# Attention of a fused two-block kernel: no weight splits on GpSimd, score copies on ScalarE, two heads' score products in turns, and a branch whose short arm comes first

## The chip, the cores and the metric

The kernel runs on one core of a Trainium2 chip. The metric is the time of one execution in device microseconds; of several runs the median counts. The trace is one profiled execution of its own; its engines are PE (TensorE), PEld (its weight loads), DVE (VectorE), ACT (ScalarE), POOL (GpSimd) and SP (SyncE, which issues most of the transfers).

## The reference, cut to what matters

One sequence of 256 positions, 1024 wide, goes through two blocks. The first mixes with a gated delta rule, a sparse attention and a pooling mixer, and has a feed-forward part with 4096 hidden columns. The second is modulated by a condition vector (six vectors of 1024 from `cond @ ada_w`), has a stick-breaking attention of 16 heads of width 64, and a mixture of 32 experts of which each position takes two; a root-mean-square norm ends it. The change is in the attention and behind the experts. What the attention computes:

```python
mod = cond @ ada_w[i] + ada_b[i]
sh1, sc1, g1, sh2, sc2, g2 = jnp.split(mod[:, None, :], N_MOD, axis=-1)
h = rms_norm_2(x, norm_g[i, 0]) * (1.0 + sc1) + sh1
...
z = jnp.einsum('bhqd,bhkd->bhqk', q_blk, k, preferred_element_type=jnp.float32) * scale
causal = kpos[None, :] < qpos[:, None]
log_keep = jnp.where(causal, jax.nn.log_sigmoid(-z), 0.0)
suffix = lax.cumsum(log_keep, axis=3, reverse=True) - log_keep
a = jnp.where(causal, jnp.exp(jax.nn.log_sigmoid(z) + suffix), 0.0)
return jnp.einsum('bhqk,bhkd->bhqd', a.astype(v.dtype), v)
```

## The kernel before, in words

Every large weight is read from memory in tiles of 1 MB into a ring (`ring`, issued on SP). The dense products want nearly full float32 precision, so `split` cuts each weight half-tile of 128x1024 in two parts: `whi`, a rounded copy made by ScalarE (L278), and `wlo = w - whi` (L279), made by VectorE, or, while `self.share` is set, by GpSimd and VectorE in alternation. TensorE then makes three products per piece (hi·hi, lo·hi, hi·lo: L340 to L342 in `dense`, L373 to L375 in `dense_T`, L400 to L402 in `dense_out`). `ffn` sets `self.share` at its very end (L1326), so the splits of the attention alternate.

`stick` is the attention. `proj(c)` runs over six chunks of 512 columns of the input projection in the order v, qk, qk, qk, v, qk. A v chunk leaves `sv` by two VectorE copies (L1373); a qk chunk leaves `sq` by ScalarE (L1378) and `sk` by VectorE (L1379). `score(j)` works on two heads, which lie in rows 0 to 63 and 64 to 127 of one `sq`/`sk` tile. For each head, one after the other, it makes a 256-column product, a 128-column product and adds the mask by a product with the identity (L1387, L1388, L1390). Each head has its own 512 columns of the tile `z`. Then VectorE makes the scaled copy `zs` (L1393), ScalarE makes Abs, Exp and Ln (L1395 to L1397), VectorE makes `ze` (L1398), ScalarE `zehi` (L1400), and GpSimd (for j below 6) or VectorE makes `zelo` (L1401). After that the cumulative sum is a product with a triangular matrix into `c` (L1405 to L1407), VectorE subtracts it (L1408) and ScalarE takes Exp (L1409). `value(j)` multiplies with v (L1418, L1419); here the two heads write different column halves (64 output rows each). `hilo` makes `ohi` and `olo` (L919, L920).

Scores of j = 0 to 5 are made between the projection chunks. Those of j = 6 and 7 are mixed into the output projection (`dense_out`, order of `SB_END`), which is called the tail below. `res` and the sums over squares follow, then routing and the experts.

Beside the attention, the modulation of the second half is made: `self.side` (L1423) holds eight pieces of work (`ada`, quarters 4 and 5, four tiles each), and every weight tile that a dense loop takes pops one entry (`beside`), the first four being empty. A piece is a 1 MB tile and four VectorE operations `ada` (L1218), and the last piece of a quarter adds a few products (L1228).

The order of instructions on each engine is fixed in the program; a scheduler has set it by priority, and in the last part, the tail, it is the order of the code.

The experts' part is called through `If(level < 33)`. The near arm walks 28 positions of experts (each 6 MB of weights) and calls `ends(rest)`: the last sums, the norm, the output (`sums`, `finish`: four transfers, all issued on SP, L2015), then a load of the size of the next position into a register on the engines and a second branch (`If(nv > 0)`, L1983) for the positions that are hardly ever filled. In the traced execution that body is skipped.

Of the kernel before, what the change touches and what calls it, by code (L numbers as in the profile page):

```python
# [8 lines left out]
F32 = mybir.dt.float32  # L9
# [191 lines left out]
class Kern:  # L201
# [1045 lines left out]
    def ffn(self):  # L1247
        nc, a = self.nc, self.a
        with self.tc.tile_pool(name="ffn", bufs=2, reuse_waits="tile") as pool:
# [75 lines left out]
            self.more_split()  # L1325
            self.share = True  # L1326

# [7 lines left out]
    def stick(self):  # L1335
        nc, a = self.nc, self.a
        hT = self.sT
        with self.tc.tile_pool(name="sb", bufs=1, reuse_waits="tile") as pool:
# [23 lines left out]
            def proj(c):  # L1362
                kind, ix = SB_CHUNKS[c]
                off = c * D * 512
                if kind == "v":
                    outs = [self.ps("mm") for _ in range(2)]
                    if c == 0:
                        self.warm(EDGE, "z")
                    self.dense(a["sb_w_in"], off, 512, 2, hT, outs, lead=self.last_T if c == 0 else None)
                    if c == 0:  # L1370
                        self.ordered.close()
                    for i in range(2):
                        nc.vector.tensor_copy(v[ix][i], outs[i])  # L1373
                    return
                outs = [self.ps("mm", (128, 2, T)) for _ in range(2)]
                self.dense_T(a["sb_w_in"], off, 512, hT, outs)
                qT[ix], kT[ix] = [pool.tile([128, 2, T], F32, name=z, bufs=2) for z in ("sq", "sk")]
                nc.scalar.activation(qT[ix], outs[0], AF.Copy)  # L1378
                self.i_proj = nc.vector.tensor_copy(kT[ix], outs[1])  # L1379

            def score(j):

                z = self.ps("z", (128, 2, 512))
                for b in range(2):
                    par = slice(64 * b, 64 * b + 64)
                    q, k = qT[j // 2][par, j % 2], kT[j // 2][par, j % 2]
                    nc.tensor.matmul(z[:, b, 0:256], k[:, 0:128], q, start=True, stop=False)  # L1387
                    nc.tensor.matmul(z[:, b, 256:384], k[:, 128:256], q[:, 128:256], start=False, stop=False)  # L1388
                    zz = z[:, b].rearrange("p (a b) -> p a b", a=4)
                    nc.tensor.matmul(zz[:, 0:3:2], self.identb, self.neg[:, 1:2].to_broadcast([128, 2, 128]), start=False, stop=True)  # L1390
                z = z[:, :, 0:384]
                zs = pool.tile([128, 2, 384], F32, name="zs", tag="zs", bufs=4)
                nc.vector.tensor_scalar(zs, z, 0.125, None, op0=OP.mult)  # L1393
                e = pool.tile([128, 2, 384], F32, name="ze", bufs=2)
                nc.scalar.activation(e, z, AF.Abs, scale=0.125)  # L1395
                nc.scalar.activation(e, e, AF.Exp, scale=-1.0)
# [3 lines left out]
                nc.scalar.activation(hi, e, AF.Copy)  # L1400
                (nc.gpsimd if j < 6 else nc.vector).tensor_sub(lo, e, hi.bitcast(F32))  # L1401
                yield
# [19 lines left out]
            scratch = lambda: pool.tile([128, 2, 384], F32, name="ze", bufs=2).rearrange("p a b -> p (a b)")[:, 0:256]  # L1422
            self.side = [None] * 4 + [lambda q=q, b=b: ada(q, b) for q in (4, 5) for b in range(4)]  # L1423

# [99 lines left out]
    def route(self, pool):  # L1524
# [72 lines left out]
        for i in range(2):  # L1597
# [27 lines left out]
        self.level = c.tile([1, 1], I32, name="level")  # L1625
        nc.vector.scalar_tensor_tensor(self.level, self.eid[:, 1, BIG:BIG + 1], 32.0,
                                       self.eid[:, 1, BIG + MID:BIG + MID + 1], op0=OP.subtract, op1=OP.max)
        self.slot = c.tile([128, 4, NPOS], F32, name="slot")
# [304 lines left out]
    def positions(self):  # L1933
# [4 lines left out]
        for z, p in enumerate(fixed):  # L1938
            self.job(p, 4, self.xg1, 32 * z, z, ("po", "pg"))
        level = nc.values_load(self.level, min_val=-32, max_val=128)  # L1940
        with tc.If(level < 33) as near:
# [9 lines left out]
            self.walk(order, batches, ("po", "pg"))  # L1951
            self.ends(rest)
        with near.Else():
# [48 lines left out]
    def finish(self):  # L2002

        nc, a = self.nc, self.a
        with self.in_order(mybir.EngineType.DVE):
            rstd = [self.rstd(i) for i in range(2)]
            for i, r in enumerate(rstd):
                for n in range(2):
# [4 lines left out]
                    else:  # L2013
                        nc.vector.scalar_tensor_tensor(y, self.x[:, i, cc], r, self.fg[:, cc], op0=OP.mult, op1=OP.mult)
                    nc.sync.dma_start(a["out"][128 * i:128 * i + 128, cc], y)  # L2015

# [52 lines left out]
```

## Time and profile before

| | us |
|---|---|
| runs | 1034.55, 1035.42, 1038.5; median 1035.42 |
| profiled execution | 1031.82 |
| its span, first to last instruction | 1030.0 |
| mean granted clock of TensorE | 0.975 of full speed |
| PE / DVE / ACT / POOL busy | 931.6 / 617.2 / 375.1 / 140.1 |
| attention, from the first v product to the last value product | about 409 to 539 |
| experts | about 560 to 1014 |
| last output transfers issued | 1018.2 to 1022.6 |

The shares of the page are averages over stages with different limits, so each stage is read by itself: which engine is full there, what ends the waits of that engine, and whether a gain there can reach the end.

### The profile page before, as it was taken

The page shows a single profiled execution, that of the slowest core. Times are in us where ns is not written, and L with a number is a line of the kernel's source. Part 1 is how long each engine was busy: PE and PEld are TensorE (multiplying, and loading weights), DVE is VectorE, ACT ScalarE, POOL GpSimd, SP SyncE. Part 2 cuts the span into 40 slices and gives each one's busy share as a digit, 9 for nine tenths or more (in the row PEclk, how much of TensorE's full clock was granted, in tenths as well). Part 3 has the DMA queues.
Part 4 walks back from the last instruction along what each step waited for, and adds up shares of the span by engine and source line. Part 5 has one row for each costly group of instructions (what it writes and reads, how often), then busy time and mean ns, then how long its engine had stood idle before and what let it go on. Part 6 is the DMA issues. An engine that isn't in the chain of part 4 may idle for free.

```text
span 1030.0 us, 16215 instructions
## 1 busy us (share of the span) xinstructions
PE 931.6 (90%) x6318; PEld 618.2 (60%) x6318; DVE 617.2 (60%) x1077; ACT 375.1 (36%) x661; POOL 140.1 (14%) x108
## 2 busy tenths in 40 slices
PE   8999998999999999999898988888788899988873
PEld 6766866778899897997766553333244334434331
DVE  5977767459777655587746764454445252545443
ACT  6574344455445555465452222111122111111112
POOL 4426420201000003444410000000000000000001
PEclk9999999999999999999899999999999999999997
DMA  9641051688968844465748899999999999999992
GB/s 326 233 155 61 23 205 42 244 328 297 393 253 294 316 171 165 170 252 198 269 158 305 314 366 374 423 420 420 420 421 421 422 420 422 419 421 421 421 421 110
DMA packets 47076, 306.74 MB, mean 298 GB/s; under 512 B 6138, under 2 KB 7170, under 8 KB 12040
## 3 DMA queue, kind: packets, MB, share of 16 engines
q1 hardware_dynamic: 46696, 304.43, 75.2%
q8 instruction: 54, 0.88, 0.4%
q10 hardware_dynamic: 288, 1.11, 0.3%
q14 instruction: 38, 0.31, 0.1%
HBM read 304.47 MB, written 1.06 MB: 297 GB/s over the span
## 4 chain that ended last, share of the span: by engine, by line
PE 65%; DMA 16%; DVE 12%; ACT 4%; issue 2%; SPq 0%; POOL 0%; DVEq 0%; ACTq 0%
DMA ring<-in_moe_w_dram 15%; PE t L1787 8%; PE py L1845 5%; PE mm L373 4%; PE mm L374 4%; PE mm L375 4%; PE pg L1783 3%; PE g L340 3%; PE g L341 2%; PE g L342 2%; PE mm L1700 2%; PE po L1875 2%; DVE cacc L667 2%; PE mm L342 1%; DVE ada L1218 1%
## 5 line engine op out<-in xcount | busy, mean ns | idle before, releaser
L278 ACT ACTIVATE whi<-ring 128x1024 fp32r<-128x1024 f32 (+2 forms) x129 | 134.1, 1044 | 113.8 <-PE mm L375 53.8
L279 DVE TENSOR_TENSOR wlo<-ring,whi 128x1024 fp32r<-128x1024 f32 (+2 forms) x99 | 127.5, 1290 | 71.6 <-ACT whi L278 70.5
L1787 PE MATMUL t<-ring,xg 128*32 128x256 f32 (+1 forms) x1632 | 139.6, 409 | 4.4 <-DMA ring<-in_moe_w_dram 4.4
L1787 PEld LDWEIGHTS t<-ring,xg 128*32 128x32 f32 (+1 forms) x1632 | 54.5, 113 | 72.9 <-issue 37.6
L1845 PE MATMUL py<-ring,ht 128*32 128x512 f32 (+2 forms) x488 | 85.1, 628 | 11.8 <-DMA ring<-in_moe_w_dram 7.7
L279 POOL TENSOR_TENSOR wlo<-ring,whi 128x1024 fp32r<-128x1024 f32 (+1 forms) x30 | 73.9, 2464 | 109.6 <-ACT whi L278 94.5
L1868 ACT ACTIVATE yhi<-y 128x512 fp32r<-128x512 f32 x64 | 40.3, 630 | 121.1 <-DVE y L1867 117.8
L1218 DVE SCALAR_TENSOR_TENSOR ada<-ring,cs,ada 128x512 f32<-128x512 f32 x96 | 75.9, 829 | 1.5 <-DMA ring<-in_ada_w_dram 1.5
L1867 DVE TENSOR_TENSOR y<-py,g 128x512 f32<-128x512 f32 x64 | 44.1, 689 | 51.7 <-PE py L1845 51.3
L1812 ACT ACTIVATE silu<-t 128x128 f32<-128x128 f32 (+1 forms) x30 | 8.9, 298 | 166.9 <-PE t L1787 166.9
L2000 POOL TENSOR_TENSOR out<-x,fg 128x512 f32<-128x512 f32 x2 | 2.9, 1448 | 459.8 <-DVE x L1650 459.8
L1650 DVE SCALAR_TENSOR_TENSOR x<-po,slot,x 128x512 f32<-128x512 f32 x63 | 47.1, 748 | 22.5 <-PE po L1875 22.3
L1872 DVE TENSOR_TENSOR ylo<-y,yhi 128x512 fp32r<-128x512 f32 x64 | 44.1, 688 | 24.3 <-ACT yhi L1868 23.6
L1650 DVE SCALAR_TENSOR_TENSOR x<-pg,slot,x 128x512 f32<-128x512 f32 x64 | 46.5, 743 | 7.5 <-PE pg L1875 7.5
L1845 PEld LDWEIGHTS py<-ring,ht 128*32 128x32 f32 (+2 forms) x488 | 20.7, 121 | 48.5 <-issue 33.9
L1813 DVE TENSOR_TENSOR silu<-silu,t 128x128 f32<-128x128 f32 (+1 forms) x30 | 9.4, 313 | 66.9 <-ACT silu L1812 66.9
L340 PE MATMUL g<-whi,fhi 128*128 128x512 f32 x112 | 43.6, 397 | 1.4 <-ACT whi L278 1.4
L341 PE MATMUL g<-wlo,fhi 128*128 128x512 f32 x112 | 43.9, 392 | 0.0
L342 PE MATMUL g<-whi,flo 128*128 128x512 f32 x112 | 43.6, 389 | 0.0
L1875 PE MATMUL po<-yhi,ohT 128*128 128x512 f32 x63 | 30.6, 485 | 13.0 <-ACT yhi L1868 11.8
L1875 PEld LDWEIGHTS po<-yhi,ohT 128*128 128x128 f32 x63 | 12.1, 192 | 44.2 <-ACT yhi L1868 29.4
L1820 PE MATMUL mm<-ident,silu 128*128 128x128 f32 x44 | 11.6, 307 | 25.0 <-DVE silu L1813 25.0
(569 smaller groups left out, 2161.2 us busy)
## 6 DMA issues: line engine op xcount, KB each, us to landing
ring<-in_moe_w_dram SPq DMA_DIRECT2D x183, 1024.0 KB, 19.7
ring<-in_w_ffn_dram SPq DMA_DIRECT2D x32, 1024.0 KB, 8.2
ring<-in_ada_w_dram SPq DMA_DIRECT2D x24, 1024.0 KB, 5.0
ring<-in_sb_w_in_dram SPq DMA_DIRECT2D x12, 1024.0 KB, 4.9
ring<-in_w_in_dram SPq DMA_DIRECT2D x8, 1024.0 KB, 8.4
ring<-in_cmp_w_dram SPq DMA_DIRECT2D x4, 1024.0 KB, 4.8
ring<-in_w_out_dram SPq DMA_DIRECT2D x4, 1024.0 KB, 7.0
ring<-in_sb_w_out_dram SPq DMA_DIRECT2D x4, 1024.0 KB, 4.8
```

Source lines behind the costliest of these rows:

```text
L278: nc.scalar.activation(hi[:, c], w[:, c], AF.Copy)
L279: eng.tensor_sub(lo[:, c], w[:, c], hi[:, c].bitcast(F32))
L340: nc.tensor.matmul(outs[i], lh.at(k, tk), h, start=st, stop=False)
L341: nc.tensor.matmul(outs[i], lh.at(k, tk), l, start=False, stop=False)
L342: nc.tensor.matmul(outs[i], ll.at(k, tk), h, start=False, stop=sp)
L1218: nc.vector.scalar_tensor_tensor(acc[:, cc], w[:, 512 * j:512 * j + 512], self.cs[:, k:k + 1], acc[:, cc], op0=OP.mult, op1=OP.add)
L1650: self.nc.vector.scalar_tensor_tensor(x, y, gate, x, op0=OP.mult, op1=OP.add)
L1787: self.nc.tensor.matmul(t[1][C * j:C * j + C], x, wq[:, :, W * j:W * j + W], start=kt == 0, stop=kt == 7)
L1845: nc.tensor.matmul(py[n][C * j:C * j + C], hT[:, b, C * j:C * j + C], w[n][f // 2][:, 512 * (f % 2):512 * (f % 2) + 512], start=b == 0, st ...
L1867: nc.vector.tensor_mul(t, py[n], self.g2[:, cc[n]])
L1872: (nc.gpsimd if split else nc.vector).tensor_sub(y[1][:, cc[n]], t, y[0][:, cc[n]].bitcast(F32))
L1875: nc.tensor.matmul(ps, ohT[:, 128 * i:128 * i + 128], y[z][:, cc[n]], start=z == 0, stop=z == 1)
```

## The change

1. `self.share = True` at the end of `ffn` goes: all `wlo` of the attention are made by VectorE.
2. In `proj`, the first half of a v chunk is copied by ScalarE. The factor 0.125 moves into the copy `sq`. `self.i_proj`, behind which the pieces of `ada` are placed, is now also set by a v chunk.
3. In `score`, the two heads' 256-column products come first, then the two 128-column products, then the two masks. The copy `zs` is made by ScalarE behind Abs for j below 6, by VectorE for j = 6 and 7. `zelo` is always made by VectorE.
4. The eight pieces of `ada` go to other weight tiles: quarter 4 beside tiles 2, 4, 6 and 8, quarter 5 beside 9, 10, 11 and 13, where they stood beside tiles 4 to 11.
5. `level` takes one more operation, so that a filled position behind the 28 also leads to the other arm. The near arm then ends with `sums` and `finish`, with no register load and no second branch.
6. In `finish`, the two first halves of the output are issued on SP and the two second halves on ScalarE's queue.

```diff
             self.more_split()
-            self.share = True
...
-                    for i in range(2):
-                        nc.vector.tensor_copy(v[ix][i], outs[i])
+                    nc.scalar.activation(v[ix][0], outs[0], AF.Copy)
+                    self.i_proj = nc.vector.tensor_copy(v[ix][1], outs[1])
                     return
...
-                nc.scalar.activation(qT[ix], outs[0], AF.Copy)
+                nc.scalar.activation(qT[ix], outs[0], AF.Copy, scale=0.125)
...
+                q, k = [[t[j // 2][64 * b:64 * b + 64, j % 2] for b in range(2)] for t in (qT, kT)]
                 for b in range(2):
-                    par = slice(64 * b, 64 * b + 64)
-                    q, k = qT[j // 2][par, j % 2], kT[j // 2][par, j % 2]
-                    nc.tensor.matmul(z[:, b, 0:256], k[:, 0:128], q, start=True, stop=False)
-                    nc.tensor.matmul(z[:, b, 256:384], k[:, 128:256], q[:, 128:256], start=False, stop=False)
+                    nc.tensor.matmul(z[:, b, 0:256], k[b][:, 0:128], q[b], start=True, stop=False)
+                for b in range(2):
+                    nc.tensor.matmul(z[:, b, 256:384], k[b][:, 128:256], q[b][:, 128:256], start=False, stop=False)
+                for b in range(2):
                     zz = z[:, b].rearrange("p (a b) -> p a b", a=4)
                     nc.tensor.matmul(zz[:, 0:3:2], self.identb, self.neg[:, 1:2].to_broadcast([128, 2, 128]), start=False, stop=True)
...
-                nc.vector.tensor_scalar(zs, z, 0.125, None, op0=OP.mult)
                 e = pool.tile([128, 2, 384], F32, name="ze", bufs=2)
-                nc.scalar.activation(e, z, AF.Abs, scale=0.125)
+                nc.scalar.activation(e, z, AF.Abs)
+                if j < 6:
+                    nc.scalar.activation(zs, z, AF.Copy)
+                else:
+                    nc.vector.tensor_copy(zs, z)
...
-                (nc.gpsimd if j < 6 else nc.vector).tensor_sub(lo, e, hi.bitcast(F32))
+                nc.vector.tensor_sub(lo, e, hi.bitcast(F32))
...
-            self.side = [None] * 4 + [lambda q=q, b=b: ada(q, b) for q in (4, 5) for b in range(4)]
+            side = {z: (4, b) for b, z in enumerate((2, 4, 6, 8))}
+            side.update({z: (5, b) for b, z in enumerate((9, 10, 11, 13))})
+            self.side = [(lambda q=side[z][0], b=side[z][1]: ada(q, b)) if z in side else None for z in range(14)]
...
+        nc.vector.scalar_tensor_tensor(self.level, size(32 - NFIX), 33.0, self.level, op0=OP.mult, op1=OP.max)
...
-            self.ends(rest)
+            self.sums()
+            self.finish()
...
-                    nc.sync.dma_start(a["out"][128 * i:128 * i + 128, cc], y)
+                    (nc.sync, nc.scalar)[n].dma_start(a["out"][128 * i:128 * i + 128, cc], y)
```

The order of the instructions, at three places. First TensorE at the first pair of heads, in the second qk chunk (`z` is the score tile, `mm` the projection's result, `neg` and `identb` the mask). Before:

```order
L375 MATMUL mm_4248<-sloa_3852,whi_4289 128x256
L1387 MATMUL z_4187<-sq_4183,sk_4184 128x256
L1388 MATMUL z_4187<-sq_4183,sk_4184 128x128
L1390 LDWEIGHTS identb_87
L1390 MATMUL z_4187<-neg_97,identb_87 128x2x128
L1387 MATMUL z_4187<-sq_4183,sk_4184 128x256
L1388 MATMUL z_4187<-sq_4183,sk_4184 128x128
L1390 LDWEIGHTS identb_87
L1390 MATMUL z_4187<-neg_97,identb_87 128x2x128
L373 MATMUL mm_4249<-shia_3850,whi_4261 128x256
```

The same place of the changed kernel:

```order
L375 MATMUL mm_4257<-sloa_3852,whi_4295 128x256
L1386 MATMUL z_4196<-sq_4192,sk_4193 128x256 x2
L1388 MATMUL z_4196<-sq_4192,sk_4193 128x128 x2
L1391 LDWEIGHTS identb_87
L1391 MATMUL z_4196<-neg_97,identb_87 128x2x128
L1391 LDWEIGHTS identb_87
L1391 MATMUL z_4196<-neg_97,identb_87 128x2x128
L373 MATMUL mm_4258<-shia_3850,whi_4267 128x256
```

The six products of the pair stand in the same place between the projection's products; the products of equal shape, one of each row half, now follow each other.

Next VectorE up to the copy of the second v chunk (`sv10`, `sv11`), which frees the tiles that the last qk chunk writes. Before:

```order
L1408 TENSOR_TENSOR zs_4426<-zs_4426,c_4437 128x768
L1218 SCALAR_TENSOR_TENSOR ada_4663<-ring_4767,cs_136,ada_4663 128x512
L1393 TENSOR_SCALAR zs_4605<-z_4598 128x768
L920 TENSOR_TENSOR olo_3953<-po_4446,ohi_3952 128x256
L1218 SCALAR_TENSOR_TENSOR ada_4663<-ring_4767,cs_136,ada_4663 128x512 x3
L279 TENSOR_TENSOR wlo_4802<-ring_4765,whi_4801 128x1024
L1218 SCALAR_TENSOR_TENSOR ada_4663<-ring_4831,cs_136,ada_4663 128x512
L1373 COPY sv10_3936<-mm_4659 128x512
L1218 SCALAR_TENSOR_TENSOR ada_4663<-ring_4831,cs_136,ada_4663 128x512
L1373 COPY sv11_3937<-mm_4660 128x512
```

The same stretch of the changed kernel:

```order
L279 TENSOR_TENSOR wlo_4768<-ring_4759,whi_4767 128x1024
L1218 SCALAR_TENSOR_TENSOR ada_4697<-ring_4700,cs_136,ada_4697 128x512 x2
L1402 SCALAR_TENSOR_TENSOR ze_4589<-zs_4588,ze_4589 128x768
L279 TENSOR_TENSOR wlo_4796<-ring_4759,whi_4795 128x1024
L1218 SCALAR_TENSOR_TENSOR ada_4697<-ring_4700,cs_136,ada_4697 128x512
L920 TENSOR_TENSOR olo_3953<-po_4608,ohi_3952 128x256
L1218 SCALAR_TENSOR_TENSOR ada_4697<-ring_4700,cs_136,ada_4697 128x512
L1448 TENSOR_REDUCE sw_4745<-junk_4742 128x36
L1405 TENSOR_TENSOR zelo_4596<-ze_4589,zehi_4595 128x768
L1372 COPY sv11_3937<-mm_4643 128x512
```

`wlo` and `zelo` stand here now, which GpSimd made before; `zs` and `sv10` are gone to ScalarE; five `ada` stood ahead of the first copy, four do now, with other work between them.

Last SP where the near arm ends (`out_0_dram` is the result, the `TENSOR_LOAD` behind the branch belongs to what is skipped). Before:

```order
L1734 DMA ring_8911<-in_moe_w_dram 128x2048
L2015 DMA out_0_dram<-out_8959 128x512 x4
L1983 COMPARE_AND_BRANCH
L1986 TENSOR_LOAD eid_5397
L1986 ISA x2
```

The same end of the changed kernel:

```order
L1741 DMA ring_8912<-in_moe_w_dram 128x2048
L2023 DMA out_0_dram<-out_8960 128x512 x2
L1948 UNCONDITIONAL_BRANCH
L1982 TENSOR_LOAD eid_5397
L1982 ISA x2
```

SP issues two output transfers in the place of four (ScalarE has the other two) and jumps over the other arm straight behind them, where it had a conditional branch of its own for the rest.

## Rows read from the trace of the kernel before

**Rows 1.** The page: busy time, share of the span, instructions of each engine.

```profile
PE 931.6 (90%) x6318; PEld 618.2 (60%) x6318; DVE 617.2 (60%) x1077; ACT 375.1 (36%) x661; POOL 140.1 (14%) x108
```

**Rows 2.** Windows: length, PE, PEld, DVE, ACT, POOL busy, clock, DMA share, GB/s.

```profile
418.00:513.60 95.60, 92.89 (x619) 81.05 (x619) 71.04 (x77) 52.28 (x64) 44.73 (x21) 0.96 0.62 224
513.60:540.00 26.40, 25.00 (x126) 18.37 (x126) 13.94 (x16) 13.67 (x18) 4.77 (x2) 1.00 0.45 155
700.00:800.00 100.00, 85.20 (x631) 36.89 (x631) 48.48 (x89) 19.59 (x44) 0.00 (x0) 0.97 1.01 421
```

**Rows 3.** Timeline of SP's queue behind the attention: start, duration, what.

```profile
566.29 2.66 SPq L1734 DMA_DIRECT2D ring<-in_moe_w_dram  x2
```

**Rows 4.** Waits of PE, 404 to 545 us: total, times, longest.

```profile
PE mm L373 <- DVE sv L1373: 2.7, 1, 2.7
...
PE c L1407 <- DVE zelo L1401: 0.9, 1, 0.9
PE z L400 <- ACT ze L1395: 0.5, 1, 0.5
```

**Rows 5.** Windows around the longest of these waits.

```profile
490.00:495.00 5.00, 2.29 (x12) 1.66 (x11) 5.00 (x6) 0.96 (x2) 3.12 (x3) 0.86 0.59 202
495.00:500.00 5.00, 5.00 (x25) 5.00 (x25) 5.00 (x8) 0.84 (x1) 0.71 (x1) 0.50 0.83 288
```

**Rows 6.** Timeline of DVE, 476 to 495 us.

```profile
476.86 1.21 DVE L279 TENSOR_TENSOR wlo<-ring,whi 128x1024 fp32r<-128x1024 f32 x1
478.00 1.40 DVE L1218 SCALAR_TENSOR_TENSOR ada<-ring,cs,ada 128x512 f32<-128x512 f32 x2
...
484.85 6.22 DVE L1218 SCALAR_TENSOR_TENSOR ada<-ring,cs,ada 128x512 f32<-128x512 f32 x3
...
493.67 0.68 DVE L1373 COPY sv<-mm 128x512 f32<-128x512 f32 x1
```

**Rows 7.** Timeline of PE around the first pair of heads.

```profile
436.53 0.28 PE L374 MATMUL mm<-shia,wlo 128*128 128x256 f32 x1
436.65 0.28 PE L375 MATMUL mm<-sloa,whi 128*128 128x256 f32 x1
436.86 0.70 PE L1387 MATMUL z<-sq,sk 64*128 64x256 f32 x2
437.39 0.38 PE L1388 MATMUL z<-sq,sk 64*128 64x128 f32 x2
437.70 0.28 PE L1390 MATMUL z<-neg,identb 128*128 128x256 bf16 x1
...
438.81 0.36 PE L373 MATMUL mm<-shia,whi 128*128 128x256 f32 x1
```

**Rows 8.** Timeline of PE at one value product of two heads.

```profile
462.34 0.66 PE L1418 MATMUL po<-zs,sv 128*64 128x256 f32 x4
...
463.14 0.63 PE L1228 MATMUL t<-ada,one 128*32 128x256 f32 x7
```

**Rows 9.** Groups of DVE, 404 to 545 us: count, busy, mean ns, idle before.

```profile
L1218 DVE SCALAR_TENSOR_TENSOR ada<-ring,cs,ada 128x512 f32<-128x512 f32 x32 | 30.8, 1001 | 0.0
L279 DVE TENSOR_TENSOR wlo<-ring,whi 128x1024 fp32r<-128x1024 f32 x16 | 25.6, 1601 | 12.6 <-ACT whi L278 12.6
L1393 DVE TENSOR_SCALAR zs<-z 128x768 f32<-128x768 f32 x8 | 7.6, 953 | 8.6 <-PE z L1390 7.6 <-issue 1.0
```

**Rows 10.** Groups of POOL, 404 to 545 us.

```profile
L279 POOL TENSOR_TENSOR wlo<-ring,whi 128x1024 fp32r<-128x1024 f32 x16 | 40.5, 2530 | 46.3 <-ACT whi L278 38.8 <-issue 7.4
L1401 POOL TENSOR_TENSOR zelo<-ze,zehi 128x768 fp32r<-128x768 f32 x6 | 11.1, 1845 | 20.8 <-ACT zehi L1400 20.8
```

**Rows 11.** Timeline of SP's queue at the end.

```profile
1018.21 4.40 SPq L2015 DMA_DIRECT2D out_dram<-out  x4
```

**Rows 12.** DMA busy tenths, 1015 to 1031 us in 40 slices of 0.4 us.

```profile
DMA  0010000000999612993279330100000000000000
```

**Rows 13.** Waits of SP's queue, 1010 to 1031 us.

```profile
SPq L1983 <- SPq L1983: 2.8, 1, 2.8
```

More of the change, by code (lines that the diff above doesn't have):

```diff
@@ L1625, in route @@
         self.level = c.tile([1, 1], I32, name="level")
-        nc.vector.scalar_tensor_tensor(self.level, self.eid[:, 1, BIG:BIG + 1], 32.0,
-                                       self.eid[:, 1, BIG + MID:BIG + MID + 1], op0=OP.subtract, op1=OP.max)
+        size = lambda p: self.eid[:, 1, p:p + 1]
+        nc.vector.scalar_tensor_tensor(self.level, size(BIG), 32.0, size(BIG + MID), op0=OP.subtract, op1=OP.max)
+        nc.vector.scalar_tensor_tensor(self.level, size(32 - NFIX), 33.0, self.level, op0=OP.mult, op1=OP.max)
         self.slot = c.tile([128, 4, NPOS], F32, name="slot")
@@ L1939, in positions @@
             self.job(p, 4, self.xg1, 32 * z, z, ("po", "pg"))
-        level = nc.values_load(self.level, min_val=-32, max_val=128)
+        level = nc.values_load(self.level, min_val=-32, max_val=33 * 128)
         with tc.If(level < 33) as near:
```

## The prediction, made before the changed kernel was run

> **What bounds the kernel now.** I read the page's shares first, then the stages by windows, then the waits of the full engine in the stage that the change touches. The page says that PE is busy 90% of the span and DVE 60% [rows 1]. That is an average. In the attention, from 418 us to the first product of the output projection at 513.6, PE is busy 92.9 of 95.6 us, DVE 71.0, ACT 52.3, POOL 44.7, and the transfers have a share of 0.62 [rows 2]: PE bounds it, and what shortens PE's queue or PE's waits shortens the stage. From 700 us on the transfers run at 1.01 and 421 GB/s [rows 2]: the experts' weights bound that part, and nothing in it changes. The experts' loads start behind the attention: the next ring loads go out at 566.29 [rows 3], when buffers come free. So I expect a gain in the attention to move that whole stream forward by the same amount, one to one.
>
> PE's waits between 404 and 545 us are few: 2.7 us for the copy `sv`, 0.9 for `zelo`, 0.5 for `ze` [rows 4]. The 2.7 us cost more than their length. In the windows behind them the granted clock is 0.86 and then 0.50, the lower of the two levels (1.2 GHz), with PE busy all of the second window and 25 products in it [rows 5]; at full speed such products start 0.12 us apart (at 436.53 and 436.65) [rows 7]. So these 25 would have taken 3.0 us in place of 5.0: 2.0 lost there, and some 0.6 more on both sides of that window. The wait and what the clock did after it cost 2.7 + 2.6 = 5.3 us. Its cause is on DVE: three `ada` take 6.22 us there, where two alone take 1.40, and the copy `sv` comes behind them at 493.67 [rows 6].
>
> **The change part by part.** *GpSimd's splits go away.* `ada` takes 1.00 us in the mean, 0.70 alone; `wlo` on DVE 1.60 in the mean, 1.21 alone [rows 6, 9]. GpSimd does 16 `wlo` and 6 `zelo` in that time at 2.53 and 1.85 us [rows 10]. I take it that the two engines slow each other. DVE's bill for 418 to 513.6, beginning at 71.0 [rows 2]: 28 `ada` by 0.30 less, -8.4; 11 `wlo` by 0.39 less, -4.3; six `zs` to ACT at 0.95 [rows 9], -5.7; two `sv` at 0.68, -1.4; 12 `wlo` from GpSimd at 1.21, +14.5 (POOL's 21 instructions there less 6 `zelo` and 3 small ones); six `zelo`, a row of the same shape as `zs`, at 0.95, +5.7. That is 71.4 us. The stage, if the rest of this sum holds, is 95.6 - 10.4 = 85.2 us long, so DVE is 84% busy where it was 74%. ACT gets six copies and two halves of v; at DVE's prices that is 7.1 us on 52.3, or 70% of the stage. PE does not wait for either on the average, but DVE has little slack, in the chunks with two pieces of `ada` above all.
>
> *The long wait.* In the order on DVE, the first v half is now copied by ACT, four `ada` stand ahead of the second in place of five, each at 0.70 and with shorter work between. From 484.85 to 493.67 DVE worked 8.8 us through five instructions; the same at their prices alone is 4 x 0.70 + 1.21 + 0.70 = 4.7, so the 2.7 us of wait are covered by 4.1 us. I book the whole 5.3 as gained.
>
> *New waits on DVE.* The copies `sk`, the `zelo` and the `wlo` now queue on one engine behind `ada`; PE is queued behind each of them, and the experts' loads behind PE. The trace shows none of these waits. The bounds are nothing, and one such stall as the one above, 5.3 us; I take 2.0, nearer to the small waits of 0.5 and 0.9 [rows 4], of which it is about three.
>
> *Scores in turns.* A pair of heads takes 438.81 - 436.86 = 1.95 us: per head 0.53 for the 256 columns, 0.31 for the 128, and the mask [rows 7]. The two heads use different row halves of the array and different columns of `z`. If equal products of the two halves run side by side, a pair takes 0.53 + 0.31 + two masks with 0.11 to 0.15 each, about 1.1 us: 0.85 less. The row nearest to that is the value product: four passes of 256 columns and four of 128 for two heads, which write different column halves, take 463.14 - 462.34 = 0.80 us [rows 8], when a head alone, by the score's rows, would take 0.84; so two heads there cost no more than one. No row shows it for row halves alone. The bounds are 0 and 0.85 for each of the eight pairs. I take 0.85: six pairs before the output projection make 6 x 0.85 = 5.1.
>
> The Trainium skill, "TensorE: Matmul & The Clock Gate", Part 3, says that matmuls in distinct row groups run at the same time and start about 4 ns apart; by it the pair would save the 0.85 us. The trace agrees for column halves only.
>
> *The tail.* It takes 26.4 us, PE is busy 25.0 of it [rows 2]. Its two pairs save 1.7; the waits of 0.5 and 0.9 there [rows 4] go with the faster DVE: 3.1. Against that stand the seven column sums of `ada` that the fifth quarter brings in (about 0.6, L1228 [rows 8]), and a wait for the copy `zs`, which now comes behind `wlo` and `ada` on DVE (0 to 1): +2.0 is left, between 0 and 3.1.
>
> *The level's extra operation* is one more on a single element in a chain before the experts: 0.15 us at most and beside loads that are under way. The pieces of `ada` that move bring their 1 MB loads along on SP, past projection tiles; the transfers are at 0.62 there [rows 2], which hides them. If not, a tile comes late by its own transfer, some 2.5 us at 421 GB/s.
>
> *The end.* SP issues four outputs from 1018.21 for 4.40 us [rows 11]; the transfers come in two bursts with a gap between, up to 1025.4 [rows 12]. Then SP's own branch takes 2.8 us [rows 13], and the span ends at 1030.0, 4.6 us behind the last transfer: 1.8 is left for the rest. In the changed kernel SP jumps behind two issues, at about 1018.4 + 2.2 = 1020.6, and is through at 1023.4 while transfers run; these end between 1022.2 (no gap) and 1025.4 (as now). The later of the two plus 1.8 is 1025.2 to 1027.2: a gain of 2.8 to 4.8. I take 3.8.
>
> *The sum.* 5.3 + 5.1 - 2.0 + 2.0 + 3.8 = 14.2 us. The profiled execution took 1031.82 (its span and 1.8 around it): 1017.6. The median of the runs is 3.6 above it: 1035.42 - 14.2 = 1021.2.
>
> **The rivals.** *A, row halves run one after the other.* Then the pairs save nothing: 14.2 - 5.1 - 1.7 = 7.4, so 1028.0. For it: no row shows row halves together. Against it: the column halves do [rows 8].
>
> *B, DVE becomes the bound.* At 84% in the mean it is over 100% in some chunk; a copy is late, PE pauses, and the clock falls as at 491. The place is the same, the copies `sk` and `sv` behind `ada` and `wlo`; the price is 5.3 each, in place of my 2.0. Two such stalls give 14.2 + 2.0 - 10.6 = 5.6, so 1029.8; three 0.3, so 1035.1; from the fourth on the kernel is slower: 5.0 lost, 1040.4. For it: DVE is busy all of 490 to 500 now [rows 5]. Against it: the single-engine prices are lower than those that made that stall.
>
> *C, the end does not pay.* ScalarE's own issue, or another engine's jump, ends last in place of SP's branch. Then the end brings only what the transfers gain by the second queue, 1.0, and the time is 1024.0. For it: every engine has to jump over the other arm. Against it: only SP issues transfers behind its last wait now.
>
> **How the numbers follow.** My forecast, all terms together, has a chance of 0.60; its own range goes from 5.3 + 5.1 + 3.1 + 4.8 = 18.3 gained (1017.1) to 5.3 + 5.1 - 5.3 + 0 + 2.8 = 7.9 (1027.5). A has 0.17, C 0.08, B with two or three stalls 0.11, and B with four or more 0.04. The range reaches a little below the forecast's own, since the runs before lie 4 us apart, and up to B's two stalls: 1014 to 1030; left out are most of B and a little on the low side, under 0.2. About 0.5%, 5.2 us, is what a measurement can tell from no change. Faster than that are the forecast, A, C and a little of B, 0.87; within it the rest of B's smaller case, 0.09; slower its larger one, 0.04.
>
> **What the profile after would show.** Scores: the first rows of a pair would start within some 0.02 us of each other, and a pair would take about 1.1 us. GpSimd: `ada` at 0.70 and `wlo` at 1.21 on DVE throughout. The long wait: no wait for `sv` above 1 us, and a granted clock of 1.0 through the attention. New waits: those of PE on DVE's `sk`, `zelo` and `wlo` sum to 2 us; above 5 with a clock of 0.5 behind them would be B. The stream: the next ring loads at about 556 in place of 566.29, and the last expert's product earlier by the same 10.4. The end: no branch row of SP behind the last transfer, and some 8 us from SP's first output issue to the end, in place of 1030.0 - 1018.2 = 11.8. It would be wrong if the gain of the attention were not seen again at the ring loads, or if PE waited more than before.

## The result, and the profile after

The changed kernel takes 1018.38 us in the median (1015.95 to 1019.1, 4 runs) against 1034.99 before (1032.95 to 1038.5, 4 runs). The ratio is 0.983, with a 95% interval of 0.980 to 0.985: 1.7% faster, some 17 us. The forecast was 1021.2, and the time lies within its range.

The span of the profiled execution is 1016.9 us where it was 1030.0. The stretches below show where the 13.1 us between these two spans are. I measure the attention from the start of the first product that waits for `sloa` (L342) to the start of the last value product; to that product's end, as the first expectation below counts it, it is 0.2 to 0.3 us more.

| us | before | after |
|---|---|---|
| start of the attention | 409.7 | 414.1 |
| attention | 129.0 | 115.5 |
| next ring loads of the experts on SP | 566.3 | 557.1 |
| from there to SP's first output issue | 451.9 | 452.7 |
| first output issue to the end of the span | 11.8 | 7.1 |

The attention gave 13.6 us and the end 4.7. Against that the attention started 4.4 us later, behind code that the change does not touch; what this is stands in the last section. The experts' part took the same time to 0.8 us and moved as a whole. 13.6 + 4.7 - 4.4 - 0.8 makes the 13.1.

The page's first part, in the form of [rows 1], then the windows before and behind the first product of the output projection, in the form of [rows 2]:

```profile
PE 925.4 (91%) x6318; PEld 611.1 (60%) x6318; DVE 617.2 (61%) x1092; ACT 379.5 (37%) x669; POOL 88.3 (9%) x86
```

```profile
422.30:505.80 83.50, 82.93 (x614) 73.90 (x613) 66.31 (x82) 55.08 (x70) 2.84 (x3) 1.00 0.59 211
505.80:529.80 24.00, 22.66 (x130) 16.39 (x128) 17.93 (x22) 14.10 (x19) 0.00 (x0) 1.00 0.82 308
```

The stage is PE's still, 82.9 of 83.5 us, and now at a granted clock of 1.00 where it was 0.96. DVE has 66.3 us of work there, and 4 us more than before in the tail.

PE's waits, 404 to 535 us, and DVE's two groups, to be read against [rows 4] and [rows 9]:

```profile
PE c L1411 <- DVE zelo L1405: 1.0, 2, 0.6
PE mm L342 <- DVE sloa L546: 0.8, 1, 0.8
PE z L1386 <- DVE zs L1399: 0.8, 1, 0.8
PE po L1450 <- DVE sw L1448: 0.2, 1, 0.2
```

```profile
L279 DVE TENSOR_TENSOR wlo<-ring,whi 128x1024 fp32r<-128x1024 f32 x32 | 39.0, 1219 | 14.9 <-ACT whi L278 14.7
L1218 DVE SCALAR_TENSOR_TENSOR ada<-ring,cs,ada 128x512 f32<-128x512 f32 x32 | 22.9, 744 | 0.0
```

The wait for `sv` is gone. VectorE makes 32 splits in 39.0 us, where it took 25.6 us for 16 of them; `ada` is down from 1.00 to 0.74 us.

A pair of heads on PE, in the form of [rows 7] (x4 are the passes of both heads):

```profile
507.25 0.70 PE L1386 MATMUL z<-sq,sk 64*128 64x256 f32 x4
507.79 0.39 PE L1388 MATMUL z<-sq,sk 64*128 64x128 f32 x4
508.11 0.39 PE L1391 MATMUL z<-neg,identb 128*128 128x256 bf16 x2
508.26 0.48 PE L400 MATMUL mm<-whi,ohi 128*128 128x512 f32 x1
```

The four 256-column passes of two heads take 0.54 us, as long as the two passes of one head took before, and the first passes of the two heads start 6 ns apart in the trace: the row halves run side by side. The pair takes 508.26 - 507.25 = 1.01 us in place of 1.95.

The queues at the end, in the form of [rows 11]:

```profile
1009.82 2.00 SPq L2023 DMA_DIRECT2D out_dram<-out  x2
1009.85 1.96 ACTq L2023 DMA_DIRECT2D out_dram<-out  x2
```

The branch row of [rows 13] has no counterpart: SP's only waits there are for ScalarE's output and, at the very end, for the other engines.

### The profile page after: what moved, and what is told of

The parts are those of the page before. It is cut to its first block, busy times and chain, and to the rows that moved or that the text cites. A ratio compares the mean times of both kernels' runs of the same rounds, so it can differ in the third digit from the quotient of the medians.

```text
span 1016.9 us, 16191 instructions
## 1 busy us (share of the span) xinstructions
PE 925.4 (91%) x6318; PEld 611.1 (60%) x6318; DVE 617.2 (61%) x1092; ACT 379.5 (37%) x669; POOL 88.3 (9%) x86
## 4 chain that ended last, share of the span: by engine, by line
PE 70%; DVE 14%; DMA 7%; ACT 6%; issue 2%; SPq 0%; ACTq 0%; POOL 0%; DVEq 0%
PE t L1794 11%; DMA ring<-in_moe_w_dram 6%; PE py L1852 6%; PE mm L373 4%; PE mm L374 4%; PE mm L375 4%; PE po L1882 3%; PE pg L1790 3%; PE mm L1707 3%; PE g L340 3%; PE g L341 3%; PE g L342 3%; DVE y L1874 2%; PE pg L1882 2%; DVE x L1657 2%
## 5 line engine op out<-in xcount | busy, mean ns | idle before, releaser
L279 DVE TENSOR_TENSOR wlo<-ring,whi 128x1024 fp32r<-128x1024 f32 (+2 forms) x115 | 140.5, 1224 | 74.2 <-ACT whi L278 73.9
L1218 DVE SCALAR_TENSOR_TENSOR ada<-ring,cs,ada 128x512 f32<-128x512 f32 x96 | 68.1, 743 | 2.2 <-DMA ring<-in_ada_w_dram 2.2
L342 PE MATMUL g<-whi,flo 128*128 128x512 f32 x112 | 43.6, 389 | 0.0
L1882 PEld LDWEIGHTS po<-yhi,ohT 128*128 128x128 f32 x63 | 12.1, 192 | 45.5 <-ACT yhi L1875 34.4
L279 POOL TENSOR_TENSOR wlo<-ring,whi 128x1024 fp32r<-128x1024 f32 (+1 forms) x14 | 33.6, 2398 | 64.0 <-ACT whi L278 56.4
```

The costliest lines, as they stand in the source:

```text
L279: eng.tensor_sub(lo[:, c], w[:, c], hi[:, c].bitcast(F32))
L342: nc.tensor.matmul(outs[i], ll.at(k, tk), h, start=False, stop=sp)
L1218: nc.vector.scalar_tensor_tensor(acc[:, cc], w[:, 512 * j:512 * j + 512], self.cs[:, k:k + 1], acc[:, cc], op0=OP.mult, op1=OP.add)
L1882: nc.tensor.matmul(ps, ohT[:, 128 * i:128 * i + 128], y[z][:, cc[n]], start=z == 0, stop=z == 1)
```

## The experiments

Two theories stood against each other. Mine: contention with GpSimd makes the long wait, PE's products bound the rest, so each term of the sum adds to the others. The rival: one part is the whole (the turns, or the new places of `ada`), and the rest rides along. Every ratio below is against the kernel before on the same chip; the two stretches are each read from one trace.

| kernel | median us | ratio, 95% interval | attention us | output issue to end us |
|---|---|---|---|---|
| before | 1034.99 | 1 | 129.0 | 11.8 |
| changed | 1018.38 | 0.983 (0.980 to 0.985) | 115.5 | 7.1 |
| heads apart | 1025.34 | 0.989 (0.986 to 0.993) | 121.5 | 6.8 |
| GpSimd back | 1024.66 | 0.988 (0.985 to 0.992) | 126.0 | 7.0 |
| `ada` where it was | 1021.60 | 0.986 (0.983 to 0.990) | 121.0 | 6.8 |
| before, no GpSimd | 1031.41 | 0.995 (0.992 to 0.997) | 122.8 | 13.8 |
| before, turns | 1036.57 | 1.001 (0.999 to 1.004) | 127.6 | 11.4 |
| before, both | 1022.20 | 0.988 (0.985 to 0.991) | 115.5 | 13.0 |
| end undone | 1021.90 | 0.988 (0.984 to 0.991) | 115.5 | 11.8 |
| one queue | 1018.44 | 0.983 (0.980 to 0.986) | 115.5 | 7.6 |
| `zs` on VectorE | 1015.47 | 0.980 (0.978 to 0.983) | 116.5 | 6.9 |
| `zs` all on ScalarE | 1016.38 | 0.983 (0.980 to 0.985) | 114.6 | 7.0 |
| last piece late | 1015.65 | 0.982 (0.979 to 0.984) | 115.2 | 7.3 |
| spread, not late | 1030.89 | 0.996 (0.993 to 0.998) | 127.4 | 7.6 |

The attention's length is the sharper measure: the three kernels in which it has the same program (changed, end undone, one queue) agree within 0.1 us, while their times scatter by several us. The last column scatters more: 6.8 to 7.6 us among the kernels with the short branch, whether on one queue or two, and 11.4 to 13.8 among those with the end of before.

**Heads apart.**

```diff
 for b in range(2):
     nc.tensor.matmul(z[:, b, 0:256], k[b][:, 0:128], q[b], start=True, stop=False)
-for b in range(2):
     nc.tensor.matmul(z[:, b, 256:384], k[b][:, 128:256], q[b][:, 128:256], start=False, stop=False)
-for b in range(2):
     zz = z[:, b].rearrange("p (a b) -> p a b", a=4)
```

> The changed kernel with one part undone: the score products stand head by head again. The attention, from the first third product (the wait for sloa) to the last value product, takes 115.7 us in the changed kernel and 129.2 before. If the row halves running side by side give 0.94 us per pair, it goes back to 115.7 + 8 x 0.94 = 123.2, and the time to about 1026. If the turns are worth little and the rest of the change brought the gain, it stays at 116 to 118, and the time at 1018 to 1020.

The attention took 121.5 us, 6.1 more; the time went up by 0.6%. The turns carry that part, less than the 7.5 of eight pairs, since 1.4 us of PE's waits are gone in this kernel: 0.8 for `zs`, 0.4 for `zelo` and 0.2 for `sw`.

**GpSimd back.**

```diff
             self.more_split()
+            self.share = True
...
-                nc.vector.tensor_sub(lo, e, hi.bitcast(F32))
+                (nc.gpsimd if j < 6 else nc.vector).tensor_sub(lo, e, hi.bitcast(F32))
```

> The changed kernel with GpSimd back at alternate splits and at zelo for j below 6; all else as changed. If GpSimd and VectorE working together made the long wait, ada goes back to about 1.0 us in the mean, wlo on VectorE to 1.6, PE waits for VectorE or GpSimd by 3 us or more in the attention, and the time is 1021 to 1025. If the new places of ada and ScalarE's share of the copies ended the wait, it is 1017 to 1020 with no wait above 1 us.

The attention took 126.0 us. PE's longest waits in it, and `ada` on DVE:

```profile
PE z L400 <- DVE zs L1400: 2.5, 1, 2.5
PE po L1423 <- DVE modc L1238: 1.9, 1, 1.9
PE c L1410 <- ACT zehi L1405: 1.2, 2, 1.0
```

```profile
L1218 DVE SCALAR_TENSOR_TENSOR ada<-ring,cs,ada 128x512 f32<-128x512 f32 x32 | 38.5, 1236 | 4.4 <-DMA ada<-in_ada_b_dram 4.4
```

VectorE has less work in number here (16 splits and 2 `zelo` in place of 32 and 8), yet each `ada` takes 1.24 us in place of 0.74. The waits came back, at other places. PE waited for none of GpSimd's own results before [rows 4]. So the contention is a cause by itself, whichever wait it lands on.

How the two engines slow each other can be read from the trace of the kernel before. GpSimd beside the three `ada` of [rows 6] that begin at 484.85:

```profile
484.66 2.40 POOL L279 TENSOR_TENSOR wlo<-ring,whi 128x1024 fp32r<-128x1024 f32 x1 [8.27 <-ACT whi L278]
487.98 2.53 POOL L279 TENSOR_TENSOR wlo<-ring,whi 128x1024 fp32r<-128x1024 f32 x1 [0.93 <-ACT whi L278]
```

The three `ada` took 2.77, 0.74 and 2.87 us. The first and the third began while GpSimd was at work, and each ended 0.56 us behind the end of GpSimd's instruction; the second began in the gap between the two. So VectorE was not slowed evenly, it waited GpSimd's instruction out. All five `ada` above 0.75 us in this attention, and all eleven in the kernel with GpSimd back, began beside a GpSimd instruction and ended 0.55 or 0.56 us behind it; the ten `wlo` on VectorE above 1.25 us in these two traces ended 1.08 or 1.09 us behind it. The copies `sk` and `sv` and the scaled copy `zs` that began so, which read PSUM, took 0.69, 0.68 and 0.96 us at most, as alone.

**Before, no GpSimd.**

```diff
-            self.share = True
...
-                (nc.gpsimd if j < 6 else nc.vector).tensor_sub(lo, e, hi.bitcast(F32))
+                nc.vector.tensor_sub(lo, e, hi.bitcast(F32))
```

> The kernel before with one part of the change alone: no wlo and no zelo on GpSimd, while VectorE keeps all zs and sv copies and ada stays where it was. VectorE's work before the output projection is then about 71.4 + 5.7 + 1.4 = 78.5 us of some 90, 87%. If contention was the cause, the long wait (5.3 us with its clock) goes and small waits of 1 to 3 us come: 1030 to 1033. If VectorE becomes the bound without ScalarE's help, PE waits for it by 5 us or more and the time is 1034 to 1040.

The attention took 122.8 us, 6.2 less, with `ada` where it was and all copies on VectorE. All of PE's waits in it:

```profile
PE mm L342 <- DVE sloa L546: 0.8, 1, 0.8
PE c L1406 <- DVE zelo L1400: 0.6, 1, 0.6
PE z L400 <- ACT ze L1394: 0.5, 1, 0.5
```

The long wait is gone by this part alone, and the granted clock is 1.00 throughout the attention. VectorE was able to take all of GpSimd's work with no help from ScalarE.

**Before, turns.**

```diff
+q, k = [[t[j // 2][64 * b:64 * b + 64, j % 2] for b in range(2)] for t in (qT, kT)]
 for b in range(2):
-    par = slice(64 * b, 64 * b + 64)
-    q, k = qT[j // 2][par, j % 2], kT[j // 2][par, j % 2]
-    nc.tensor.matmul(z[:, b, 0:256], k[:, 0:128], q, start=True, stop=False)
-    nc.tensor.matmul(z[:, b, 256:384], k[:, 128:256], q[:, 128:256], start=False, stop=False)
+    nc.tensor.matmul(z[:, b, 0:256], k[b][:, 0:128], q[b], start=True, stop=False)
+for b in range(2):
+    nc.tensor.matmul(z[:, b, 256:384], k[b][:, 128:256], q[b][:, 128:256], start=False, stop=False)
+for b in range(2):
```

> The kernel before with one part of the change alone: the two heads' score products in turns. Eight pairs by 0.94 us make 7.5 us if PE bounds the whole attention: 129.0 goes to 121.5, and the time to 1028. If VectorE's chain of ada and splits sets the time of the long wait, what is saved ahead of it (five pairs, 4.7 us) becomes a longer wait there: the attention takes 124 to 127 us and the time is 1030 to 1033.

Even less came of it: 1.4 us in the attention, and nothing in the time. PE's two longest waits, and the windows around the first:

```profile
PE mm L373 <- DVE sv L1373: 4.6, 1, 4.6
PE z L400 <- ACT ze L1396: 2.7, 1, 2.7
```

```profile
490.00:495.00 5.00, 1.27 (x6) 1.27 (x7) 5.00 (x7) 0.00 (x0) 1.92 (x2) 0.75 0.72 241
495.00:500.00 5.00, 5.00 (x26) 4.36 (x25) 5.00 (x5) 0.85 (x1) 1.82 (x1) 0.57 0.68 247
```

PE reached the place sooner and waited for the same copy `sv`: 4.6 us in place of 2.7 [rows 4], with VectorE busy throughout, and in the tail the wait for `ze` went from 0.5 to 2.7, with a granted clock of 0.82 and 0.84 in the windows at 520 and 525 us, where the tail had 1.00 before [rows 2]. A saving on PE ahead of a wait for VectorE is turned into wait.

**Before, both.** The two diffs above together.

> The kernel before with two parts of the change: the score products in turns, and no wlo and no zelo on GpSimd. Alone the turns left the time as it was (ratio 1.001) and the freed GpSimd brought 5.6 us. If the turns are worth their 6 to 7 us as soon as the wait for sv is gone, the attention takes 129.0 - 6.2 - 6.1 = 117 us and the time is about 1023. If VectorE, which still has all zs and sv copies, swallows them, the attention stays at 121 to 123 and the time at 1028 to 1030.

115.5 us, the same as the changed kernel. So 129.0 - 6.2 = 122.8 by the freed GpSimd, and 7.4 more by the turns, which is eight pairs by 0.94 to 0.2 us. The score copies on ScalarE, the v half and the new places of `ada` together bring nothing to the attention beyond these two. In time this kernel and the one with the end undone, which both lack the short end, have the same ratio, 0.988.

**End undone.**

```diff
-        nc.vector.scalar_tensor_tensor(self.level, size(32 - NFIX), 33.0, self.level, op0=OP.mult, op1=OP.max)
...
-            self.sums()
-            self.finish()
+            self.ends(rest)
...
-                    (nc.sync, nc.scalar)[n].dma_start(a["out"][128 * i:128 * i + 128, cc], y)
+                    nc.sync.dma_start(a["out"][128 * i:128 * i + 128, cc], y)
```

> The changed kernel with the end of the kernel before: level without the extra operation, a register load and a second branch behind the output, all four outputs issued on SP. From SP's first output issue to the end of the span it took 11.8 us before and 7.1 in the changed kernel. If the end is worth what the two traces differ by, it goes back to 11.5 to 12 us and the time to about 1023; the attention stays at 115 to 117 us. If the difference is chance, it stays near 7 us.

**One queue.** The last of these edits alone.

> The changed kernel with all four outputs issued on SP, the branch as changed. If the branch is the larger part of the end's gain (2.8 of 4.7 us), the stretch from the first output issue to the end is 8.5 to 9.5 us and the time 1019 to 1021. If the second queue is the larger part, it is 10 us or more.

SP's output issues, first with the end undone (span 1020.6 us), then with one queue (span 1018.6), and SP's branch in the former:

```profile
1008.78 3.61 SPq L2021 DMA_DIRECT2D out_dram<-out  x4
```

```profile
1011.01 2.70 SPq L2023 DMA_DIRECT2D out_dram<-out  x4
```

```profile
SPq L1989 <- SPq L1989: 3.2, 1, 3.2
```

Undone, the end takes 1020.6 - 1008.8 = 11.8 us; with the short branch and one queue 7.6, less than either case expected; with two queues 7.1. Of the 4.2 us between the first two, 0.9 is SP's four issues (3.61 against 2.70), which the branch does not explain. From the last issue's end to the end of the span it is 8.2 us with the second branch and 4.9 without: 3.3, about the 3.2 of the branch row. The 0.5 of the second queue lies within the scatter of 6.8 to 7.6 and is not shown. The time agrees for the whole end (0.988 against 0.983, with intervals that overlap a little) and cannot tell the queue.

**Score copies on VectorE.**

```diff
-                if j < 6:
-                    nc.scalar.activation(zs, z, AF.Copy)
-                else:
-                    nc.vector.tensor_copy(zs, z)
+                nc.vector.tensor_copy(zs, z)
```

> The changed kernel with all score copies zs on VectorE. VectorE gets six copies by 0.95 us more, some 77 us of the 92 before the output projection. If it has slack enough, the attention stays within 1 us of 115.5 and the time at 1018 to 1020. If VectorE is near its limit without ScalarE's help, PE's waits for it grow by 2 to 5 us, with a lower clock behind a wait above 2 us, and the time is 1021 to 1025.

116.5 us, 1.1 more, and a time that can't be told from the changed kernel's. VectorE has slack; moving these copies was not needed.

**The places of `ada`.** Three kernels.

```diff
-            side = {z: (4, b) for b, z in enumerate((2, 4, 6, 8))}
-            side.update({z: (5, b) for b, z in enumerate((9, 10, 11, 13))})
...
+            self.side = [None] * 4 + [lambda q=q, b=b: ada(q, b) for q in (4, 5) for b in range(4)]
```

> The changed kernel with the eight pieces of ada beside the weight tiles 4 to 11 again. If the contention with GpSimd made the long wait, it stays away: ada at 0.70 us, waits of PE under 2 us in sum, 1017 to 1020. If the places of ada made it, a wait of 2 us or more with the clock at 0.5 behind it comes back, 1023 to 1025.

Neither: no wait at `sv`, but 121.0 us, with a new wait of 3.6 us in the tail and a granted clock of 0.74 and 0.92 in the windows at 515 and 520 us. ScalarE at that place, in this kernel and then in the changed one:

```profile
513.17 0.84 ACT L1404 ACTIVATE zehi<-ze 128x768 fp32r<-128x768 f32 x1 [1.34 <-DVE ze L1402]
513.92 1.04 ACT L278 ACTIVATE whi<-ring 128x1024 fp32r<-128x1024 f32 x1
514.87 0.79 ACT L1395 ACTIVATE ze<-z 128x768 f32<-128x768 f32 x1
```

```profile
513.35 0.81 ACT L1395 ACTIVATE ze<-z 128x768 f32<-128x768 f32 x1 [0.60 <-PE z L1391]
514.05 0.84 ACT L1404 ACTIVATE zehi<-ze 128x768 fp32r<-128x768 f32 x1
```

and PE, which needs the tile `z` again:

```profile
517.23 0.64 PE L400 MATMUL z<-whi,ohi 128*128 128x512 f32 x1 [3.58 <-DVE zs L1399]
```

In this kernel's order the Abs of the last pair stands behind `zehi` of the pair ahead of it, and `zehi` waits for VectorE. `z` comes free when Abs and the copy `zs` have read it. VectorE's order is turned with it: here `zs` stands behind `zelo` and a split, in the changed kernel it starts at 514.19, ahead of `zelo`.

```profile
514.05 0.96 DVE L1405 TENSOR_TENSOR zelo<-ze,zehi 128x768 fp32r<-128x768 f32 x1 [0.91 <-ACT zehi L1404]
514.99 1.23 DVE L279 TENSOR_TENSOR wlo<-ring,whi 128x1024 fp32r<-128x1024 f32 x1
516.14 0.95 DVE L1399 COPY zs<-z 128x768 f32<-128x768 f32 x1
```

To see whether this order is the cause, I moved single pieces, which turn the order round.

```diff
-            side = {z: (4, b) for b, z in enumerate((2, 4, 6, 8))}
-            side.update({z: (5, b) for b, z in enumerate((9, 10, 11, 13))})
+            side = {z: (4, b) for b, z in enumerate((4, 5, 6, 7))}
+            side.update({z: (5, b) for b, z in enumerate((8, 9, 10, 13))})
```

> The changed kernel with seven pieces of ada beside the tiles 4 to 10 as before, and only the eighth beside tile 13 as changed. With all eight as before the attention took 121.0 us, with a wait of 3.6 us for zs in the tail, where ScalarE has the Abs of the last pair behind zehi of the pair ahead of it; in this kernel Abs stands ahead of zehi again. If that order made the wait, it is gone and the attention takes 116 to 117.5 us, the time 1018 to 1020. If the spreading of the seven other pieces was the gain, it stays at 120 or more, and the time at 1021 to 1023.

115.2 us and no such wait: seven pieces where they were cost nothing; the eighth decides. On ScalarE Abs stands ahead of `zehi` again.

```diff
-            side.update({z: (5, b) for b, z in enumerate((9, 10, 11, 13))})
+            side.update({z: (5, b) for b, z in enumerate((9, 10, 11, 12))})
```

> The changed kernel with its spread places of ada but the eighth piece beside tile 12 in place of 13; ScalarE's order in the tail is then that of the kernel with all eight pieces as before (zehi, then a split, then Abs). If that order makes the wait, 3 us or more of it for zs come back in the tail, the attention takes 119 to 121 us and the time is 1021 to 1023. If the spread is what counts, it stays within 1 us of 115.5 and the time at 1018 to 1020.

It was worse than either theory had it: 127.4 us. The wait for `zs` came back at 3.6, and another with it. PE at that place, then DVE:

```profile
508.44 1.53 PE L1228 MATMUL t<-ada,one 128*32 128x256 f32 x8 [4.82 <-DMA spare<-in_moe_w_dram]
```

```profile
506.31 1.22 DVE L279 TENSOR_TENSOR wlo<-ring,whi 128x1024 fp32r<-128x1024 f32 x1
507.44 1.41 DVE L1218 SCALAR_TENSOR_TENSOR ada<-ring,cs,ada 128x512 f32<-128x512 f32 x2
```

The column sums of `ada` (L1228) now stand ahead of the tail on PE and need the last `ada`, which VectorE, busy without a gap, reaches at 507.44. The row names a transfer as the releaser; the first of the two `ada` ends at 508.19, just before the products start at 508.44, so I read the wait as one for `ada`. In the changed kernel VectorE is as late with it, but the column sums stand behind the second pair, at 514.64. One tile's place cost 12 us: the two waits are 8.4 of it, and the lower clock (0.68 and 0.64 in the windows at 505 and 510 us, 0.88 and 0.78 at 520 and 525) accounts for at least part of the rest.

The wait for `zs` came in both kernels in which Abs of the last pair stands behind `zehi` and a split, 2.6 us behind the pair's last mask. In the kernel with all `zs` on VectorE it stands behind `zehi` too, but only 0.6 us behind the mask, and PE waits 0.7. So it is the delay of Abs that counts. The order was never changed with all pieces in their places, so that it is the order and nothing else of the pieces' places is likely and not shown.

**All score copies on ScalarE.**

```diff
-                if j < 6:
-                    nc.scalar.activation(zs, z, AF.Copy)
-                else:
-                    nc.vector.tensor_copy(zs, z)
+                nc.scalar.activation(zs, z, AF.Copy)
```

> The changed kernel with the two last score copies on ScalarE too. In the changed kernel PE waits 0.8 us for zs of the pair 6 on VectorE and 0.6 for zelo of the pair 7. If VectorE's queue makes these waits, the attention takes about 114.5 us in place of 115.5, too little to be told in the time (1016 to 1019). If ScalarE's longer queue delays zehi instead, it is 116 us or more.

114.6 us as expected, and nothing in the time that can be told. No kernel here is clearly faster than the changed one: the three whose medians lie below its own (with `zs` on either engine, or the last piece late) have intervals that overlap its interval.

## Point by point

**The long wait** was booked at 5.3 us, wait and clock. Freeing GpSimd alone shortened the attention by 6.2, some 0.5 of it in smaller waits. Right in cause and nearly in size; the single-engine prices held (1.22 for `wlo`, 0.74 for `ada` against the 0.70 assumed). The five instructions from 484.85 to 493.67 are 4.0 us at the prices used and not 4.7, which counts a sixth; the wait was covered either way.

**Scores in turns** were 0.85 a pair; 0.94 was measured, 7.4 for eight in the end. The rival A, row halves one after the other, is refuted by the pair's rows. The bound had been drawn from column halves, and the rule of the Trainium skill, "TensorE: Matmul & The Clock Gate", Part 3, agrees with the trace here: the passes of the two row halves stand in one row of x4 that is as long as x2 was.

What the sum did not say is that this term hangs on the one before it. It treated them as two amounts that add. Alone, the turns gave 1.4 us and no time; behind the freed GpSimd they gave 7.4.

**New waits on DVE** were 0.6 us ahead of the output projection (0.4 for `zelo`, 0.2 for `sw`), where 2.0 were booked.

**The tail** was booked at 2.0 and gave 1.4: from the first product of the output projection to the last value product it took 25.1 us before and 23.7 after. The waits of 0.5 and 0.9 did not go, as the term had it; 0.8 for `zs` and 0.6 for `zelo` stand there now, as much in sum. Its two pairs gave 1.9 and the column sums took 0.6 of it back. So the stretch ahead of the tail gave the rest, 12.1 us, where 5.3 + 5.1 - 2.0 = 8.4 were booked.

**DVE's load** was put at 71.4 of 85.2 us; it is 66.3 of 83.5. The 85.2 took the tail's 2.0 off this stage too; by the terms it should have been 87.2. And I left out that the moved pieces take four `ada` into the tail, which has 17.9 us of DVE where it had 13.9. So B was less near than it seemed, and the kernel with all `zs` on VectorE shows the slack. B is not without ground: in the kernel with the last piece one tile earlier PE does wait for VectorE and the clock falls, by the place of a product and not by VectorE's load.

**The places of `ada`** were costed at nothing, with the loads' cover as the reason. In the changed kernel that was right. The reason was not the point: the price lies in where the pieces' column sums then stand on PE, and, as far as is shown, in the order on ScalarE and VectorE; it ranges from nothing to 12 us.

**The end** was 3.8, measured 4.7. Of that 2.4 is SP's issues, 2.00 us for two where four took 4.40, and 2.3 what comes behind them. Behind the issues the branch was worth 2.3 us by these two traces and 3.3 by the two experiments, around its row of 2.8; for the second queue no run shows the 1.0 that rival C gave it.

**The shift of the experts** was right in kind: from the ring loads to the output 452.7 against 451.9 us. The ring loads came 9.2 us earlier and not 10.4, since 4.4 of the 13.6 were lost ahead of the attention.

In all 10.4 + 3.8 = 14.2 was forecast, 13.6 + 4.7 = 18.3 is what the two stretches of the traces gave, and 16.6 the medians. The attention was underrated by 3.2, above all since the new waits were small and the stretch of the long wait gave more than was booked. That the medians came nearer to the forecast than the stretches did is no merit of the sum: they hold the scatter ahead of the attention too.

## What to carry to other kernels

Two engines that slow each other can be worth less together than one: count what the second engine's work costs the first, in its mean time against its time alone, and look for instructions that end with the other engine's. A saving on the bounding engine ahead of a wait is no saving until the wait is gone, so test parts in pairs and not only one by one. When side work is moved, look in the program's order where its last consumer stands on the bounding engine, and what its place does to the other queues.

## What the runs showed of the hardware

Score products on two row halves of the array, with 64 rows each, ran side by side where they follow each other in the queue (1.01 us a pair), and one after the other where a full-height mask product stands between (1.95 us).

VectorE's `ada`, `wlo`, `ze` and `zelo`, which each read two tensors from SBUF, were held up beside a GpSimd instruction: the long ones began while one ran and ended 0.55 us (`ada`), 0.81 (`ze`, `zelo`) or 1.08 (`wlo`) behind its end. The copies `sk`, `sv` and `zs` from PSUM were not held up.

SP's issue of a 256 KB output took from 0.35 to 3.3 us, with no cause that the trace names: four took 4.40 us in one run [rows 11], 3.61 and 2.70 in others, and up to 5.25. So the second queue's worth is uncertain by more than it amounts to.

The scatter of the times by some 4 us comes, in part at least, from a stretch ahead of the attention in which all these kernels have the same program. The attention starts at 409.7 us before and at 414.1 after, and between 410.3 and 415.3 in the other kernels. The granted clock differs there; the window from 80 to 90 us, before and then after:

```profile
80.00:90.00 10.00, 10.00 (x45) 5.97 (x44) 8.54 (x20) 4.49 (x11) 6.86 (x5) 0.97 0.24 94
```

```profile
80.00:90.00 10.00, 10.00 (x37) 5.61 (x36) 7.03 (x16) 4.36 (x11) 8.26 (x5) 0.74 0.31 107
```

PE is busy all of it in both and starts 45 or 37 products. What sets how long the clock stays at its lower level (1.2 GHz) behind a pause was not tried. In the attention the waits of 0.5 to 1.0 us left it at 1.00, and those of 2.7, 3.6, 4.6 and 4.8 us had lower windows behind them, as had the 1.9 and 2.5 of the kernel with GpSimd back (0.66 and 0.75).
